# Sums over partitions for modulation rows: float32 matmuls on four column tiles instead of a split pair, and separate buffers for running sum and finished row

## The chip, the core and the metric

The kernel runs on one core of a Trainium2 chip. The metric is the device time of one execution in microseconds (us), as the median of several runs. A core has five engines that work side by side, each through its own queue in order: TensorE (PE in the profile, with its weight loads as PEld), VectorE (DVE), ScalarE (ACT), GpSimd (POOL) and SyncE (SP, which here only issues DMAs).

## The reference, cut to what matters

One layer of a decoder trunk, 512 tokens by 1024 channels, float32. A vector `c` of 1024 values is turned into six rows of 1024 values that shift, scale and gate the activations:

```
cs = silu(c)
mod = cs @ w_ada + b_ada                  # 1024 x 6144 weights
shift1, scale1, gate1, shift2, scale2, gate2 = split(mod, 6)
h = rmsnorm(x, norm1_g) * (1 + scale1) + shift1
...                                       # input projection, two attention mixers, gates
x = x + gate1 * (merged @ w_out)
h2 = rmsnorm(x, norm2_g) * (1 + scale2) + shift2
x = x + gate2 * conv_ffn(h2)
return rmsnorm(x, final_g)
```

The change touches how the last four rows (`gate1`, `shift2`, `scale2`, `gate2`) are computed. The first two are made elsewhere, at the start.

## The kernel before, in words

Most large products are done in three matmuls of a split form: an operand is cut into a rounded high part of type float32r (ScalarE, line 115) and a low part, the rest (VectorE, line 116), and high x high, high x low and low x high are summed in PSUM (lines 119 to 121). That is the helper `split`.

The program runs in stages: normalisation and the first six columns of the input projection (to about 55 us), then both attention mixers with the gate and branch projections (to about 293 us), then the output projection, then the gated MLP with its convolution.

In the second stage the order on TensorE is written out by hand (`manual_schedule` names the tensor engine alone); the order on VectorE, ScalarE, GpSimd and the DMA queues is set by a planner, which puts instructions in order by priority and by when its own model has their inputs and buffers ready. The hand-written order is a chain of attention steps with `fill(n)` between them. One `fill` step is one "tick": it runs one step of the projection at hand (three matmuls), runs what `after(n, ...)` put off by n ticks, and from tick 4 on at every eighth tick advances the generator `ada_rows` by one step.

`ada_rows` computes the four rows in eight halves of 512 columns. A half takes four steps. Each step loads two 128x512 pieces of `w_ada` into a tile `ra` (line 750; it shares four buffers, tag `raw`, with the other weights of this stage) and adds them to a running sum `arow`, each weighted by a column of `cs`: one TENSOR_SCALAR (line 755) for the first piece and one SCALAR_TENSOR_TENSOR (line 757) for each of the other seven. After tick 20 these have a raised priority, below that of the score and softmax instructions and above that of the splits of weights. `arow` has a single buffer (tag `sq2`). After the last piece it holds 128 partial sums per column, one per partition.

What is left is the sum over the 128 partitions. `arow` is split into `arh` and `arl` (lines 115 and 116), and one tick later `ada_spread` multiplies each with a matrix of ones, `onesr`, into a PSUM bank `pr` (lines 766 and 767, 128x512 each), which leaves the sum in every partition. ScalarE copies row 0 back into row 0 of `arow` (line 769), and GpSimd issues a DMA that writes it to `mod_rows`, a small tensor in device memory (line 770). `mod_rows` is read back by three loads: row 0 as `g1b` (line 929), used in line 967 to weight the output projection; rows 1 and 2 as columns (line 940); row 3 as `g2b` (line 929), late in the MLP.

Other names that the steps touch: `sd` (scores and probabilities of the differential attention, maxima in line 673, exponentials in line 687, combined in lines 690 to 693), `td` (their transposes, line 702), `aTh` and `aTl` (the transposes split, lines 430 and 431), `od` (the product with the values), `pA` and `ta` (a branch projection and its merge, line 796), `oa` (line 604: the product of the sliding-window attention with its values, float32 matmuls whose two heads use columns 0 to 63 and 64 to 127 of the array, that is two column tiles).

Of the kernel before, what the change touches and what calls it, by code (L numbers as in the profile page):

```python
# [8 lines left out]
F32 = mybir.dt.float32  # L9
F32R = mybir.dt.float32r  # L10
# [4 lines left out]
P = 128  # L15
D = 1024
S = 512
# [12 lines left out]
ADA_LAG = 1  # L30
# [23 lines left out]
def kernel(  # L54
# [22 lines left out]
    nc = tc.nc  # L77
# [3 lines left out]
    def pool(name, bufs=1, space=None, stack=ctx):  # L81
        kw = {} if space is None else {"space": space}
        return stack.enter_context(tc.tile_pool(name=name, bufs=bufs, reuse_waits="tile", **kw))

    cpool = pool("const")
    big = pool("big")
# [3 lines left out]
    def bank(tag, bufs, shape, name, dt=F32):  # L90
        return ps.tile(shape, dt, tag=tag, bufs=bufs, name=name)
# [7 lines left out]
    def tbank(name, shape=(P, S)):  # L99
        return bank("t", 2, list(shape), name)  # L100
# [4 lines left out]
    def raw_tile(shape, name):  # L105
        return wp.tile(shape, F32, tag="raw", bufs=4, name=name)
# [7 lines left out]
    def split(hi, lo, src):  # L114
        nc.scalar.copy(hi, src)
        nc.vector.tensor_sub(lo, src, hi.bitcast(F32))
# [14 lines left out]
    ones = cpool.tile([P, P], F32, name="ones")  # L131
# [1 line left out]
    warm = cpool.tile([P, 1], F32, name="warm")  # L133
    nc.vector.memset(warm, 0.0)
    nc.scalar.activation(warm, warm, AF.Exp)
    onesr = cpool.tile([P, P], F32R, name="onesr")
    nc.vector.tensor_copy(onesr, ones)
    mhalf = cpool.tile([P, 4], F32, name="mhalf")
    nc.gpsimd.memset(mhalf, -0.5)
    qsc = cpool.tile([P, 4], F32, name="qsc")  # L140
# [105 lines left out]
    ac, mods, wts = {}, {}, {}  # L246
# [269 lines left out]
    def after(n, fn):  # L516
        later.append([n, fn])
# [223 lines left out]
    mod_rows = tc.dram_tile([4, D], F32, name="mod_rows")  # L741

    def ada_rows():
        for idx in range(4):
            for hf in range(2):
                c0 = (2 + idx) * D + hf * S
                ac = big.tile([P, S], F32, tag="sq2", name=f"arow{idx}{hf}")
                for k in range(0, KT, 2):
                    r = raw_tile([P, 2, S], f"ra{idx}{hf}_{k}")
                    nc.sync.dma_start(r, wada[k * P : (k + 2) * P, c0 : c0 + S].rearrange("(a p) n -> p a n", p=P))  # L750
                    with tc.high_priority(offset=HP // 2) if tick[0] > ADA_EASY else ExitStack():
                        for a in range(2):
                            cc = cs[:, k + a : k + a + 1]
                            if k + a == 0:
                                nc.vector.tensor_scalar_mul(ac, r[:, a], cc)
                            else:
                                nc.vector.scalar_tensor_tensor(ac, r[:, a], cc, ac, ALU.mult, ALU.add)  # L757
                    yield
                ah = big.tile([P, S], F32R, tag="g2b0", name=f"arh{idx}{hf}")
                al = big.tile([P, S], F32R, tag="g2b1", name=f"arl{idx}{hf}")  # L760
                split(ah, al, ac)
                after(ADA_LAG, lambda idx=idx, hf=hf, ac=ac, ah=ah, al=al: ada_spread(idx, hf, ac, ah, al))

    def ada_spread(idx, hf, ac, ah, al):
        pr = tbank(f"pr{idx}{hf}")
        nc.tensor.matmul(pr, onesr, ah, start=True, stop=False)
        nc.tensor.matmul(pr, onesr, al, start=False, stop=True)
        row = ac[0:1, :]
        nc.scalar.copy(row, pr[0:1, :])  # L769
        nc.gpsimd.dma_start(mod_rows[idx : idx + 1, hf * S : (hf + 1) * S], row)  # L770


    pair_w = {}
# [26 lines left out]

    pairs, firsts, scored, probs, aTs = {}, {}, {}, {}, {}
    ada = ada_rows()
    add_head(0)
    add_head(1)
# [38 lines left out]
    for s in range(4 * DIFF_HEADS):  # L843
        h, n = divmod(s, NT)
# [621 lines left out]
    for i, (J, name) in enumerate(slots):  # L1466
# [21 lines left out]
        if i in rows_at:  # L1488
            hf = rows_at[i]
# [297 lines left out]
```

## Time and profile before

| what | value |
|---|---|
| median of 3 runs | 706.98 us (706.82 to 708.46) |
| the profiled execution | 708.24 us |
| its span, first to last instruction | 705.4 us |
| mean granted TensorE clock | 0.994 |
| second stage, 55 to 293 us | 238 us, PE busy 235.9 |
| the eight halves: first line 755, last line 770 | 68.4 us, 294.4 us |

The profile shows one execution. Busy time is per engine. A matmul's record includes its way through the pipeline, so records overlap and the distance between starts is the better measure of what one costs. A groups' line has line, engine, operation, output and inputs with shape, and then durations; a wait's line has who waited, for whom, total us, times, and the longest. In a timeline the first two columns are start and duration, and brackets behind a line hold the idle time before it and what ended it.

### The profile page before, as it was taken

What the parts mean: (1) busy time and instruction counts of PE and PEld (TensorE: products, weight loads), DVE (VectorE), ACT (ScalarE), POOL (GpSimd) and SP (SyncE); (2) the same over time, 40 slices, a digit from 0 to 9 for tenths busy, and PEclk for the clock granted to TensorE, in tenths of its full rate; (3) what the DMA queues carried; (4) which work ended last, traced back from release to release, by engine and by line L of the source; (5) the groups of instructions that cost most, each with busy time, mean ns of one, the idle gap of its engine ahead of it and who ended that gap; (6) DMA issues with size and microseconds to landing.
All of it is one profiled execution on the core that took longest, in us unless ns stands there. A gap on an engine that the chain in (4) does not pass through costs nothing. (4 is left out here: it accounts for less than half of the span.)

```text
span 705.4 us, 11197 instructions
## 1 busy us (share of the span) xinstructions
PE 685.0 (97%) x4155; PEld 597.1 (85%) x4155; DVE 578.4 (82%) x1107; ACT 383.9 (54%) x676; POOL 82.2 (12%) x100
## 2 busy tenths in 40 slices
PE   6999999999999999999999999999999999999994
PEld 6777777777787888888889999999999999888884
DVE  5998968788985766773579899888888999979996
ACT  3646766545543333431468656555555666656664
POOL 3000000000011000000030111111101102530300
PEclk9999999999999999999999999999999999999998
DMA  9983624263543774529617888786979748996803
GB/s 311 302 262 98 201 61 154 67 199 90 170 153 100 262 214 142 186 93 288 187 33 148 197 199 204 177 209 182 208 204 230 164 143 204 197 200 191 158 0 119
DMA packets 115861, 121.80 MB, mean 173 GB/s; under 512 B 4415, under 2 KB 93280, under 8 KB 115808
## 3 DMA queue, kind: packets, MB, share of 16 engines
q1 hardware_dynamic: 96894, 95.09, 42.7%
q0 software_dynamic: 18720, 25.73, 21.6%
q8 instruction: 32, 0.52, 0.3%
q10 hardware_dynamic: 194, 0.28, 0.1%
q14 instruction: 21, 0.17, 0.1%
HBM read 118.97 MB, written 2.11 MB: 172 GB/s over the span
## 5 line engine op out<-in xcount | busy, mean ns | idle before, releaser
L1126 PE MATMUL up<-t,m_whi 128*128 128x256 f32 x528 | 96.1, 283 | 0.0
L1126 PEld LDWEIGHTS up<-t,m_whi 128*128 128x128 f32 x528 | 82.3, 192 | 0.0
L1126 PE MATMUL up<-t,m_wlo 128*128 128x256 f32 x264 | 74.7, 283 | 0.1
L1126 PE MATMUL up<-bh,p_wlo 128*128 128x256 f32 x232 | 65.7, 284 | 0.7 <-DVE p_wlo L1069 0.7
L1126 PE MATMUL up<-bh,p_whi 128*128 128x256 f32 x232 | 65.6, 283 | 0.0
L1126 PE MATMUL up<-bl,p_whi 128*128 128x256 f32 x232 | 65.6, 283 | 0.0
L1126 PEld LDWEIGHTS up<-t,m_wlo 128*128 128x128 f32 x264 | 50.6, 192 | 0.3 <-DVE m_wlo L1069 0.3
L1126 PEld LDWEIGHTS up<-bh,p_wlo 128*128 128x128 f32 x232 | 44.5, 192 | 1.1 <-DVE p_wlo L1069 1.1
L1126 PEld LDWEIGHTS up<-bh,p_whi 128*128 128x128 f32 x232 | 44.5, 192 | 0.0
L1126 PEld LDWEIGHTS up<-bl,p_whi 128*128 128x128 f32 x232 | 44.5, 192 | 0.0
L757 DVE SCALAR_TENSOR_TENSOR arow<-ra,cs,arow 128x512 f32<-128x512 f32 x56 | 41.9, 747 | 2.6 <-DMA ra<-in_w_ada_dram 1.8
L1037 POOL DMA_DIRECT2D s<-in_w_up_dram x21 | 27.0, 1361 | 142.9 <-DMA s<-in_w_up_dram 78.0
L1069 DVE TENSOR_TENSOR m_wlo<-s,m_whi 128x1024 fp32r<-128x1024 f32 x31 | 37.7, 1217 | 2.0 <-ACT m_whi L1065 2.0
L1065 ACT CAST m_whi<-s 128x1024 fp32r<-128x1024 f32 x31 | 32.5, 1047 | 9.4 <-DVE s L1059 5.9
L1126 PE MATMUL up<-t,p_whi 128*128 128x256 f32 x176 | 32.2, 283 | 0.0
L687 ACT ACTIVATE sd<-sd,dmx 128x128 f32<-128x128 f32 (+3 forms) x32 | 17.8, 556 | 23.2 <-DVE dmx L685 15.9
L175 POOL TENSOR_TENSOR r<-ms,mhalf 128x1 f32<-128x1 f32 (+1 forms) x16 | 13.2, 828 | 144.7 <-DVE ms L173 74.0
L1126 PEld LDWEIGHTS up<-t,p_whi 128*128 128x128 f32 x176 | 27.4, 192 | 0.2 <-issue 0.2
L1133 ACT ACTIVATE gT<-a,cv 128x512 f32<-128x512 f32 x22 | 17.7, 813 | 17.6 <-DVE a L1168 17.3
L770 POOL DMA_DIRECT2D mod_rows<-arow x8 | 4.3, 540 | 193.7 <-ACT arow L769 193.5
L1065 ACT CAST p_whi<-wa 128x1024 fp32r<-128x1024 f32 x18 | 18.7, 1041 | 12.0 <-PE up L1126 7.2
L1126 PE MATMUL up<-t,p_wlo 128*128 128x256 f32 x88 | 24.9, 283 | 0.0
(478 smaller groups left out, 2073.0 us busy)
## 6 DMA issues: line engine op xcount, KB each, us to landing
ra<-in_w_ada_dram SPq DMA_DIRECT2D x32, 512.0 KB, 4.2
wa<-in_w_up_dram SPq DMA_DIRECT2D x22, 512.0 KB, 4.6
s<-in_w_up_dram SPq DMA_DIRECT2D x21, 512.0 KB, 5.1
s<-in_w_up_dram POOLq DMA_DIRECT2D x21, 512.0 KB, 7.0
adaw<-in_w_ada_dram SPq DMA_DIRECT2D x16, 512.0 KB, 4.9
w<-in_w_in_dram SPq DMA_DIRECT2D x12, 512.0 KB, 4.1
a<-in_w_up_dram SPq DMA_DIRECT2D x11, 512.0 KB, 4.8
b<-in_w_down_dram SPq DMA_DIRECT2D x10, 512.0 KB, 4.7
```

The source lines that it names most:

```text
L175: nc.gpsimd.tensor_tensor(r0, ms, mhalf[:, :n], ALU.pow)
L687: nc.scalar.activation(pm[m], pm[m], AF.Exp, bias=mx[:, m : m + 1], scale=slope, accum_out=lsum[:, m : m + 1])
L757: nc.vector.scalar_tensor_tensor(ac, r[:, a], cc, ac, ALU.mult, ALU.add)
L770: nc.gpsimd.dma_start(mod_rows[idx : idx + 1, hf * S : (hf + 1) * S], row)
L1037: nc.gpsimd.dma_start(dst, upblock(*blk), accum_op=ALU.add)
L1065: nc.scalar.copy(W[J, name][0], R[J, SRC[name]])
L1069: nc.vector.tensor_sub(lo, R[J, SRC[name]], hi.bitcast(F32))
L1126: nc.tensor.matmul(o[u], w[:, k, cu], b[:, k], start=name in ("p1", "m5", "p2") and k == 0 and x == 0, stop=k == 3 and x == 2, skip_group_ ...
L1133: nc.scalar.activation(grow(j), av[J][:, u], AF.Identity, bias=cv[:, 66 + j : 67 + j], scale=cv[:, 44 + j : 45 + j])
```

## The change

The running sum is summed over the partitions without a split. Four float32 matmuls, one for each 128 columns of the half, use 32 columns of the ones matrix as weights and write to a quarter of the partitions of one 128x128 bank: partitions 32g to 32g+31 all hold columns 128g to 128g+127 of the half. `tile_position=(0, 32 * g)` puts each on a column tile of its own. The copy takes the whole 128x128 bank into a tile `row` of its own, and the DMA takes partitions 0, 32, 64 and 96 of it, 128 values each. The running sum alternates between two buffers, tags `sq2` and `g2b1`; `row` has the tag `g2b0`. These two tags held `arh` and `arl` before. The matrix `onesr` goes.

```
-    onesr = cpool.tile([P, P], F32R, name="onesr")
-    nc.vector.tensor_copy(onesr, ones)
...
-                ac = big.tile([P, S], F32, tag="sq2", name=f"arow{idx}{hf}")
+                ac = big.tile([P, S], F32, tag=("sq2", "g2b1")[hf], name=f"arow{idx}{hf}")
...
-                ah = big.tile([P, S], F32R, tag="g2b0", name=f"arh{idx}{hf}")
-                al = big.tile([P, S], F32R, tag="g2b1", name=f"arl{idx}{hf}")
-                split(ah, al, ac)
-                after(ADA_LAG, lambda idx=idx, hf=hf, ac=ac, ah=ah, al=al: ada_spread(idx, hf, ac, ah, al))
-
-    def ada_spread(idx, hf, ac, ah, al):
-        pr = tbank(f"pr{idx}{hf}")
-        nc.tensor.matmul(pr, onesr, ah, start=True, stop=False)
-        nc.tensor.matmul(pr, onesr, al, start=False, stop=True)
-        row = ac[0:1, :]
-        nc.scalar.copy(row, pr[0:1, :])
-        nc.gpsimd.dma_start(mod_rows[idx : idx + 1, hf * S : (hf + 1) * S], row)
+                after(ADA_LAG, lambda idx=idx, hf=hf, ac=ac: ada_spread(idx, hf, ac))
+
+
+    def ada_spread(idx, hf, ac):
+        pr = tbank(f"pr{idx}{hf}", (P, P))
+        for g in range(4):
+            gs = slice(32 * g, 32 * g + 32)
+            nc.tensor.matmul(
+                pr[gs], ones[:, gs], ac[:, g * P : (g + 1) * P], start=True, stop=True, tile_position=(0, 32 * g)
+            )
+        row = big.tile([P, P], F32, tag="g2b0", name=f"row{idx}{hf}")
+        nc.scalar.copy(row, pr)
+        nc.gpsimd.dma_start(
+            mod_rows[idx, hf * S : (hf + 1) * S].rearrange("(g n) -> g n", g=4), row[0:P:32]
+        )
```

## The prediction, made before the change was run

> **What bounds the kernel now.** I read the page's totals first, then the busy time by stage, then single rows.
>
> ```profile
> PE 685.0 (97%) x4155; PEld 597.1 (85%) x4155; DVE 578.4 (82%) x1107; ACT 383.9 (54%) x676; POOL 82.2 (12%) x100
> ```
>
> ```profile
> 55.00:293.00 238.00, 235.89 (x1259) 187.86 (x1258) 184.47 (x457) 121.80 (x273) 11.78 (x16) 1.00 0.50 153
> ```
>
> The second is the stage in which all changed work lies (first arow operation 68.4 us, last row copy 293.5 us); its columns are start and end, length, busy time and count of PE, PEld, DVE, ACT and POOL, granted clock, DMA share and GB/s. PE is busy for 235.9 of 238 us at a clock of 1.00. DVE has 53.5 us free there, ACT 116. So what DVE and ACT save counts only where PE waits for them. A busy PE can still issue late (a 128x512 matmul is shown for 0.39 us, the next starts after 0.23), so I also took the starts of the matmul records, and from each distance to the next the ordinary one (columns at 2.4 per ns plus 0.0135 us, which gives 0.227 for 512). Over 55 to 293 us 11.5 us remain. Most is small change at switches between kinds of matmul; four holes are waits for data: 1.30 us after 143.44, 0.35 after 164.10, 0.49 after 212.55 and 0.74 after 214.57, together **2.9 us**. That is all that a faster DVE or ACT can win here.
>
> After 293 us, PE follows a hand-written order, DVE is 30% busy around 325 us, and the chain of waits begins only at 357 us. The last row is written by 296 us and read at 481.8. A shift at 293 us is therefore passed on whole, and nothing else is changed.
>
> **The change part by part.**
>
> *The matmuls on PE.* Today's pair stands in a stream of ordinary matmuls:
>
> ```profile
> 192.74 0.40 PE L121 MATMUL pga<-hThA,wga_l 128*128 128x512 f32 x1
> 192.97 0.39 PE L766 MATMUL pr<-arh,onesr 128*128 128x512 f32 x1
> 193.20 0.39 PE L767 MATMUL pr<-arl,onesr 128*128 128x512 f32 x1
> 193.44 0.40 PE L119 MATMUL pga<-hThA,wga_h 128*128 128x512 f32 x1
> ```
>
> From the start of the first pr matmul to that of the next unit 193.44 - 192.97 = 0.47 us, no more than two ordinary matmuls. Eight times: 3.7 us leave PE.
>
> What comes is four float32 matmuls with 32 weight columns and 128 moving columns. The nearest row is L604, float32 on two column tiles of 64:
>
> ```profile
> 77.89 0.39 PE L121 MATMUL pw<-hThA,w_l 128*128 128x512 f32 x1
> 78.21 1.73 PE L604 MATMUL oa<-pT,va 128*64 128x256 f32 x16
> 79.87 0.50 PE L119 MATMUL pw<-hThA,w_h 128*128 128x512 f32 x1
> 80.21 0.40 PE L120 MATMUL pw<-hTlA,w_h 128*128 128x512 f32 x1
> ```
>
> Its eight matmul calls stand in the trace as 16 records: a float32 matmul is two passes. The two tiles' records start together (78.475 and 78.480, 78.690 and 78.697), a pass of 256 columns follows the last after 0.216 us, one of 128 after 0.109. So the stream is 6 x 0.216 + 2 x 0.109 = 1.51 us. From 77.89 to 80.21 are 2.32 us; less two ordinary intervals of 0.23 that leaves 1.86, so going into column tiles and back costs 1.86 - 1.51 = **0.35 us**: 0.09 before the first record, some 0.05 in the first pass, the rest behind the last.
>
> With four tiles side by side the new group is 2 x 0.109 + 0.35 = 0.57 us, 0.10 more than today; eight times **+0.8 us**. No row shows four tiles at once. The lower end is that both passes hide in the switch, 0.40, which is -0.06 x 8 = -0.5 us. A middle end is that records go no faster than the fastest pairs of load and matmul that the trace has, one per 0.055 us (those of L604): 8 x 0.055 + 0.35 = 0.79, +0.32 x 8 = +2.6 us. The upper end is eight passes one after another: 8 x 0.109 + 0.35 = 1.22, +0.75 x 8 = +6.0 us. I take +0.8, since L604 is the only float32 column-tile row and its tiles do run together. The Trainium skill, "TensorEngine Tiling (Array Packing)", Key Properties, says that a change of tiling mode drains TensorE, which speaks against this change; the trace agrees, with 0.35 us. "TensorE: Matmul & The Clock Gate" there, Measured speedup vs the span model, has 2.38 times from three column tiles, 79% of ideal; by an estimate from that page, four would stream in 0.218 / 0.79 = 0.28 us and the sum here would be +1.2 in place of +0.8. No run here shows it.
>
> *The split, removed.*
>
> ```profile
> L115 ACT CAST arh<-arow x8: 602/622/624, 83.6 to 284.3; 128x512 fp32r<-128x512 f32 x8
> L116 DVE TENSOR_TENSOR arl<-arow,arh x8: 681/688/693, 87.7 to 285.0; 128x512 fp32r<-128x512 f32 x8
> L769 ACT COPY arow<-pr x8: 562/576/577, 108.9 to 293.5; 1x512 f32<-1x512 f32 x8
> ```
>
> 8 x 0.622 = 5.0 us leave ACT and 8 x 0.688 = 5.5 us leave DVE (durations are min/median/max in ns). The row copy becomes 128 x 128 elements. Its cost goes by elements per partition: a 128x128 cast from PSUM at 145.30 takes 0.27 us, so 8 x (0.576 - 0.27) = 2.4 us more leave ACT. The split was done 7 to 20 us before PE came to it, so PE did not wait for it; all of this is worth nothing but what it opens in the four holes.
>
> *Buffers.* With one arow tile, the next half's first operation waits for the write of the finished row:
>
> ```profile
> DVE arow L755 <- DMA mod_rows<-arow: 5.7, 4, 3.4
> ```
>
> That is 5.7 us in 4 waits on DVE, 3.4 the longest, and behind each, loaded halves pile up and DVE then runs them in a burst. The clearest burst makes the largest hole:
>
> ```profile
> 140.50 0.74 DVE L757 SCALAR_TENSOR_TENSOR arow<-ra,cs,arow 128x512 f32<-128x512 f32 x1
> ...
> 141.84 0.74 DVE L757 SCALAR_TENSOR_TENSOR arow<-ra,cs,arow 128x512 f32<-128x512 f32 x1
> ...
> 143.28 0.74 DVE L757 SCALAR_TENSOR_TENSOR arow<-ra,cs,arow 128x512 f32<-128x512 f32 x1
> ...
> 144.47 0.74 DVE L693 SCALAR_TENSOR_TENSOR sd<-sd,dls,sd 128x128 f32<-128x128 f32 x2
> ```
>
> ```profile
> 144.96 0.30 PE L702 MATMUL td<-ident,sd 128*128 128x128 f32 x1 [1.14 <-DVE sd L693]
> ```
>
> PE's transpose waits for L693, which stands behind L757. With two arow tiles, a half waits for the matmuls of the half before the last, some 25 us earlier, so these four operations run when their ra tiles land. Without the one at 143.28 the hole loses 0.74; without the one at 140.50 too, which delays the maxima that ACT waits for, it can lose all 1.30. I take 1.0. The holes after 212.55 and 214.57 have L115 (0.62 us on ACT at 208.94) and L116 (0.69 on DVE at 209.59) among the work just ahead; of their 1.23 us I take 0.5. What is late next there is ACT's exponentials. The hole after 164.10 I leave. Sum: **-1.5 us**.
>
> New waits: the row copy waits for the write of the row before, landed 20 us earlier (1.6 us to land). Behind L755, if it ever waited for PE, would stand DVE's maxima and splits; PE is long past those matmuls.
>
> *The rest.* The write has four pieces of 512 B in place of one of 2 KB. Its readers are g1b, issued right behind the fifth write and first used at 291.8 (64 us of cover), and the column loads at 251.7, used after 340; 1 us more costs nothing. If the cover were gone, it would be about 1 us once. The onesr cast (0.23 us at 1.11) stands in an idle stretch of DVE before 2.75: nothing. The order of DVE, ACT and the DMA queues in this stage is the planner's, and it can come out otherwise; I set that at 0, with 2.5 us to either side, about the sum of today's holes.
>
> **Sum.** +0.8 - 1.5 = -0.7 us. The profiled execution took 708.24 us around a span of 705.4, 0.2% above the median of 706.98; I carry the difference to the median: **706.3 us**.
>
> **The rivals.**
> *All holes close.* -2.9 + 0.8 = -2.1: 704.9 us. For it: three of four holes have arow work just ahead. Against: at 164.10 it is ACT's exponentials and DVE's own L693 that are late.
> *Four tiles don't run side by side* (slower). Mechanism: the float32 passes of the four tiles queue up at PE. Price: +6.0 - 1.5 = +4.5, 711.5 us; at the rate of the fastest pairs +2.6 - 1.5 = +1.1, 708.1 us. It makes the kernel measurably slower from a group of 0.47 + (2.1 + 1.5) / 8 = 0.92 us on, which is more than 5 of 8 passes in a row. For: two tiles are the most that a row shows. Against: those two cost no more than one.
> *The planner moves the burst.* arow work, now ready early and ahead of the weight splits, makes new holes ahead of PE: +2.5 for the new, nothing won, +0.8: 710.3 us. Against: DVE is 60% busy from 88 to 106 us, where the second half's sums would fall.
> *The buffers do nothing*, as arow operations stay paced by their loads: +0.8 - 0.5 = +0.3, 707.3 us.
>
> **How the numbers follow.** Forecast 0.46; all holes close 0.14; tiles in a row 0.08, pair rate 0.11; planner 0.13; buffers idle 0.08. The range leaves out the full row of tiles, most of the planner's case and the edge of the best: 704.3 to 709.5. A measurement can tell about 0.3%, 2.1 us, so faster means below 704.9: half of the best case, and 0.07 of the forecast's own spread to the planner's gain, 0.14. Slower means above 709.1: the row of tiles and most of the planner's case, 0.19. Same: 0.67.
>
> **What would show it.** The distance from the matmul before pr to the second one after it: 1.03 us instead of 0.93. pr records of four tiles starting within 0.02 us of each other. No DVE wait for mod_rows, and arow operations in pairs. The hole before the transpose near 143 us under 0.4 us. The prediction is wrong if pr groups take over 0.9 us, or if holes of over 1 us appear elsewhere between 55 and 293 us, or if anything after 293 us changes in length.

## The result, and the profile after

The changed kernel takes 710.46 us (median of 7, 709.07 to 712.94), the kernel before 706.97 (median of 7, 706.69 to 708.46). The ratio is 1.0047, 95% interval 1.0033 to 1.0061: **slower by 0.47%**. The forecast was 706.3, with 709.5 as the upper end of its range. The profiled execution took 712.94 us, the longest of the seven, with a span of 711.0. Another execution of the same kernel, traced later as the run `r_after` below, took 708.73 with a span of 706.8.

The totals of the page, after:

```profile
PE 686.1 (96%) x4203; PEld 594.8 (84%) x4203; DVE 572.4 (81%) x1098; ACT 376.8 (53%) x668; POOL 82.2 (12%) x100
```

and the stage of 55 to 293 us in it (start and end, length, then busy time and count of PE, PEld, DVE, ACT and POOL, granted clock, DMA share, GB/s):

```profile
55.00:293.00 238.00, 233.89 (x1289) 183.11 (x1288) 178.82 (x453) 113.17 (x264) 11.86 (x16) 1.00 0.50 151
```

DVE's work is down by 6.0 us and ACT's by 7.1, as intended. PE, which was busy for 235.9 us of this stage, is now busy for 233.9, at the same clock of 1.00. So PE waits more here although the engines that feed it have less to do.

Where the time went is read by matching each matmul of the one trace to the same matmul of the other and following the difference of their starts. In `r_after` it is -0.7 us at 62 us, +2.1 at 284 and +1.5 from 364 on. The +2.8 between 62 and 284 us is the loss. What lies outside varies from run to run: the profiled execution of after is already 2.1 us late at 45 us, `r_after` 0.7 early, in a part where the two programs differ by the `onesr` cast alone.

The holes of PE, taken as the prediction took them (distance to the next matmul less the ordinary one, those over 0.25 us, 55 to 300 us) are these:

| kernel | holes in us, with the time after which each opens | sum |
|---|---|---|
| before | 143: 1.30, 164: 0.35, 213: 0.49, 215: 0.74 | 2.9 |
| after, profiled | 55: 0.27, 127: 0.42, 142: 0.76, 147: 1.27, 188: 0.25, 192: 0.98, 217: 0.87, 220: 0.71 | 5.5 |
| `r_after` | 124: 0.41, 139: 0.65, 144: 1.23, 189: 0.98, 214: 0.88, 217: 0.71 | 4.9 |

The same six holes stand in both executions of the changed kernel, so they belong to its program. All but those at 55 and 220 us are PE's transpose `td` waiting for the probabilities (now line 691 on DVE). DVE's own waits tell why; this is the list of waits in `after` from 55 to 300 us (who waits, for whom, total us, times, longest):

```profile
DVE arow L755 <- DMA ra<-in_w_ada_dram: 22.2, 16, 3.9
...
PE td L700 <- DVE sd L691: 3.5, 5, 1.1
```

The same two waits in the kernel before:

```profile
DVE arow L757 <- DMA ra<-in_w_ada_dram: 1.8, 3, 0.8
...
PE td L702 <- DVE sd L693: 1.6, 3, 1.1
```

DVE also waited 5.7 us in 4 for the write of the row there. That wait is gone, as forecast, but 22.2 us of waits for loads have come. One of them is seen whole in the timeline of `r_after` (start, duration, engine, line; in brackets the idle time before it and what ended it). DVE's lines are complete from 121.71 on; of ACT and PE one line each is shown:

```profile
120.42 0.49 ACT L685 ACTIVATE sd<-sd,dmx 128x256 f32<-128x256 f32 x1
...
121.71 1.54 DVE L755 SCALAR_TENSOR_TENSOR arow<-ra,cs,arow 128x512 f32<-128x512 f32 x2 [2.48 <-DMA ra<-in_w_ada_dram]
123.17 0.22 DVE L688 RECIPROCAL dls<-dls 128x2 f32<-128x2 f32 x2
123.36 0.23 DVE L689 TENSOR_TENSOR dls<-dls,nlam 128x1 f32<-128x1 f32 x2
123.56 0.55 DVE L690 TENSOR_SCALAR sd<-sd,dls 128x128 f32<-128x128 f32 x2
124.02 0.74 DVE L691 SCALAR_TENSOR_TENSOR sd<-sd,dls,sd 128x128 f32<-128x128 f32 x2
...
124.51 0.30 PE L700 MATMUL td<-ident,sd 128*128 128x128 f32 x1 [0.24 <-DVE sd L691]
```

ACT is done with the exponentials of the first two blocks by 121.0 us. DVE could go on with the probabilities, but two running-sum operations stand ahead of them in its queue. They wait 2.48 us for their piece, 0.7 of it after the last exponential, and then take 1.5 us. The first probabilities are done at about 124.5, and PE has its hole of 0.41 us.

The matmuls themselves came out near the forecast. The group in the changed kernel's trace:

```profile
197.21 0.39 PE L121 MATMUL pga<-hThA,wga_l 128*128 128x512 f32 x1
197.53 0.43 PE L764 MATMUL pr<-arow,ones 128*32 128x128 f32 x8
197.88 0.50 PE L119 MATMUL pga<-hThA,wga_h 128*128 128x512 f32 x1
198.22 0.39 PE L120 MATMUL pga<-hTlA,wga_h 128*128 128x512 f32 x1
```

From 197.21 to 198.22 is 1.01 us; the same distance is 0.93 before. Within the group, the four tiles' records of one pass start within 0.02 us, and those of the second pass 0.13 us after the first.

### The profile page after: what moved, and what is told of

It is laid out like the page before. It is cut to its first block, busy times and chain, and to the rows that moved or that the text cites. A ratio compares the mean times of both kernels' runs of the same rounds, so it can differ in the third digit from the quotient of the medians.

```text
span 711.0 us, 11254 instructions
## 1 busy us (share of the span) xinstructions
PE 686.1 (96%) x4203; PEld 594.8 (84%) x4203; DVE 572.4 (81%) x1098; ACT 376.8 (53%) x668; POOL 82.2 (12%) x100
## 5 line engine op out<-in xcount | busy, mean ns | idle before, releaser
L755 DVE SCALAR_TENSOR_TENSOR arow<-ra,cs,arow 128x512 f32<-128x512 f32 x56 | 41.9, 748 | 22.6 <-DMA ra<-in_w_ada_dram 22.2
L769 POOL DMA_DIRECT2D mod_rows<-row x8 | 4.9, 612 | 212.3 <-ACT row L768 212.3
```

The lines of the kernel that those rows point to most:

```text
L769: nc.gpsimd.dma_start(mod_rows[idx, hf * S : (hf + 1) * S].rearrange("(g n) -> g n", g=4), row[0:P:32])
```

## The experiments

Five causes were weighed. A: the second buffer. B: the new matmuls and row path. C: time lost outside the stage (it fell already with the second trace, above). D: the running-sum operations and their waits in DVE's queue. E: the planner, which writes the queues of DVE and ACT anew when an instruction is changed, and wrote a worse order. The table has all times; each ratio is to the kernel before on the same chip. Holes are summed from 55 to 300 us, as above.

| run | time, us | ratio, 95% interval | holes, us |
|---|---|---|---|
| `e1_single` | 712.53 | 1.0083 [1.0069, 1.0097] | 8.1 |
| `e2_two` | 714.88 | 1.0124 [1.0105, 1.0142] | 9.4 |
| `e3_noprio` | 710.47 | 1.0056 [1.0043, 1.0068] | 6.2 |
| `e4_ahead` | 713.62 | 1.0096 [1.0080, 1.0111] | 8.3 |
| `e5_nosum` | 709.62 | 1.0036 [1.0024, 1.0048] | 4.6 |
| `e6_noread` | 719.00 | 1.0166 [1.0152, 1.0180] | 9.0 |
| `e8_pin` | 713.18 | 1.0085 [1.0068, 1.0103] | 7.8 |
| `e9_pinb` | 710.74 | 1.0049 [1.0037, 1.0061] | 5.6 |
| `e10_hold` | 706.49 | 0.9996 [0.9986, 1.0007] | 2.8 |
| `e12_holdsq` | 706.60 | 0.9993 [0.9983, 1.0003] | 3.1 |
| `e11_swap` | 730.90 | 1.0340 [1.0322, 1.0358] | 20.0 |
| `r_after` | 709.46 | 1.0041 [1.0027, 1.0055] | 4.9 |
| `e13_rest` | 714.04 | 1.0096 [1.0072, 1.0119] | 9.1 |
| `e14_sums` | 708.52 | 1.0026 [1.0016, 1.0037] | 4.6 |
| `e15_moved` | 709.70 | 1.0042 [1.0025, 1.0058] | 5.9 |

### One part of the change at a time

`e1_single` is the changed kernel with one buffer for the sums.

```
-                ac = big.tile([P, S], F32, tag=("sq2", "g2b1")[hf], name=f"arow{idx}{hf}")
+                ac = big.tile([P, S], F32, tag="sq2", name=f"arow{idx}{hf}")
```

> The changed kernel with one buffer for the running sum (tag sq2 for both halves), all else as changed. Theory A (order on DVE): the second buffer lets the planner put running-sum operations early in DVE's queue, where they wait for their own loads (22 us in 16 waits after the change, 1.8 in 3 before) and hold up the softmax behind them; with one buffer those waits fall under 6 us, the PE holes between the first stage's end and the output projection fall from 5.3 us back to about 2.9 or less, and the time is 706.5 to 708 us. Theory B (the new sum itself: column tiles, 128-row copy, write in four pieces): still 709.5 to 711 us, holes over 4.5 us. Theory C (the loss lies outside this stage, in the first 45 us, where the profiled execution lost 2.1 us, and in late loads around 345 us): between 709 and 710.5 us with the holes gone.

It took 712.53 us, 2 more than the change and above what any of the theories gave. **A alone fell**: taking the second buffer away doesn't give the time back. Its waits for `ra` are half as long (11.0 us in 8), and yet the hole ahead of `od` at 217 us is 2.18 us, where the changed kernel has 0.71.

`e2_two` is the kernel before with two buffers; the low part is left out, and the high part is multiplied twice so that PE has the same work.

```
-                ac = big.tile([P, S], F32, tag="sq2", name=f"arow{idx}{hf}")
+                ac = big.tile([P, S], F32, tag=("sq2", "g2b1")[hf], name=f"arow{idx}{hf}")
...
-                split(ah, al, ac)
+                nc.scalar.copy(ah, ac)
...
-        nc.tensor.matmul(pr, onesr, ah, start=True, stop=False)
-        nc.tensor.matmul(pr, onesr, al, start=False, stop=True)
+        for _ in range(2):
+            nc.tensor.matmul(pr, onesr, ah, start=True, stop=True)
```

> The kernel before with two buffers for the running sum (tags sq2 and g2b1); to free the second, the low part of the split is left out (the pair of 128x512 matmuls runs on the high part twice, the second overwriting the first, so the rows are sums of rounded values), and the pair, the one-row copy and the write stay. PE has the same matmuls as before; DVE has 8 x 0.69 us less. Theory A: waits of the running sum for its loads over 15 us in all, PE holes about 5 us, 708.5 to 710.5 us although nothing was added on PE. Theory B: 705.5 to 707.3 us. Theory C: within 1 us of before, or slower with the loss in the first 45 us.

714.88 us, without a column tile in it and above the ranges of A and B. A loss of this kind needs no new matmul, which speaks against **B**; what the new matmuls cost in the changed kernel itself shows only when the order is held, below. Half of A did come: with two buffers the sums wait 29.8 us for their loads here too (25.5 in 16 at line 757, 4.3 in 2 at line 755). So the second buffer lets the planner place the sums where they wait, but it isn't all of the loss.

### The running sums and their loads

`e3_noprio` takes away the raised priority of the loads and sums; `e4_ahead` traces each load one step earlier than its sums.

```
-                    with tc.high_priority(offset=HP // 2) if tick[0] > ADA_EASY else ExitStack():
+                    with ExitStack():
```

> The changed kernel without the raised priority of the running-sum operations, which then stand behind the weight splits of the same tick. Theory A: they move back in DVE's queue, their loads have landed by then, waits for loads fall under 10 us, PE holes to 3 us or less, 706.5 to 708.5 us, unless weights come late because their buffers are held longer. Theory B: 709.5 to 711 us. Theory C: 709 to 710.5 us.

```
+        ahead = load(0)
+        yield
...
-                    r = raw_tile([P, 2, S], f"ra{idx}{hf}_{k}")
-                    nc.sync.dma_start(r, wada[k * P : (k + 2) * P, c0 : c0 + S].rearrange("(a p) n -> p a n", p=P))
+                    r, n = ahead, 8 * idx + 4 * hf + k // 2 + 1
...
+                    if n < 32:
+                        ahead = load(n)
```

> The changed kernel with each load of the running sum's pieces issued one step (eight ticks) ahead of its use, so that a load has landed when its operations come up; one of the four weight buffers is then always taken. Theory A: waits for these loads under 5 us, PE holes under 3 us, 706 to 708 us; if the lost buffer makes weights late, holes appear at the projections instead, before the first matmul of a unit. Theory B: 709.5 to 711 us. Theory C: 709 to 710.5 us.

Neither helps: 710.47 and 713.62 us, with 25.0 us of waits for `ra` in 13 and 26.5 in 18. `e4_ahead` didn't do what it was made for: from 100 us on its loads go out hardly earlier than the changed kernel's, or not at all (the 11th at 121.4 us where that one has 119.7, the 14th at 146.0 and 146.7).

`e5_nosum` leaves out 56 of the 64 sum operations, 42 us of DVE's work; `e6_noread` lets the sums read a tile that is already there in place of the loaded one, so that no sum waits for a load (its sums are of other data; of the two lines changed the second is shown).

```
-                            else:
-                                nc.vector.scalar_tensor_tensor(ac, r[:, a], cc, ac, ALU.mult, ALU.add)
```

> The changed kernel without 56 of the 64 running-sum operations: only the first piece of each half is scaled, the other seven are loaded and not added (the rows are wrong). Theory D, formed after the first four runs: PE's holes are late transposes td, and these are late because running-sum operations, and their waits for loads, stand in DVE's queue between ACT's exponentials and the operation that combines the probabilities, or ahead of the maxima; in the changed kernel 9 of the 16 blocks lose time so. Without these operations: PE holes over 0.25 us sum to 1.5 us or less (5.3 in the changed kernel, 2.9 before), time 704 to 706 us. Rival, theory E: the planner's order of the rest (weight splits and the wait for GpSimd's power ahead of the probabilities) makes the holes whatever the running sum does: holes 3 us or more, 707.5 us or more.

```
...
-                                nc.vector.scalar_tensor_tensor(ac, r[:, a], cc, ac, ALU.mult, ALU.add)
+                                nc.vector.scalar_tensor_tensor(ac, hTh[k + a].bitcast(F32), cc, ac, ALU.mult, ALU.add)
```

> The changed kernel with all 64 running-sum operations, but reading tiles that already lie in the core (the input hT in place of the loaded weights, so the rows are wrong); the loads are still issued. It takes the wait for the loads away and leaves the operations. Theory D splits: if it is the waits, holes fall to 2 us or less and the time to 705 to 707 us; if it is the operations' own 0.75 us in the way, holes stay at 4 us or more and the time at 709 us or more. Theory E: 708.5 us or more, with the late blocks behind weight splits.

With 42 us less to do on DVE the kernel is still slower than before, 709.62 us. Its largest hole, 2.19 us, has no sum near it. DVE in `e5_nosum`:

```profile
212.40 0.55 DVE L429 TENSOR_TENSOR aTl<-td,aTh 128x384 fp32r<-128x384 f32 x1
212.87 1.22 DVE L116 TENSOR_TENSOR wba_l<-wba,wba_h 128x1024 fp32r<-128x1024 f32 x1
214.00 0.68 DVE L795 SCALAR_TENSOR_TENSOR ta<-ta,pA 128x512 f32<-128x512 f32 x1
214.60 1.22 DVE L116 TENSOR_TENSOR wga_l<-wga,wga_h 128x1024 fp32r<-128x1024 f32 x1
215.74 0.68 DVE L429 TENSOR_TENSOR aTl<-td,aTh 128x512 fp32r<-128x512 f32 x1
```

PE needs the last of these for `od` from 214.3 on and gets it at 216.4. Two weight splits and a merge, 2.9 us, stand between two pieces of the transposed tiles. In `e6_noread` no sum waits for a load, and it takes 719.0 us: 7 of its 12 us are lost before 62 us, where the planner now lays out the first stage otherwise; the rest are holes of PE in the second stage. **D by itself fell**: the sums and their waits make single holes, but in the orders that the planner wrote without them there are others.

`e8_pin` queues each step's sums behind the probabilities last traced (issue order, no wait); `e9_pinb` does the same to the kernel before.

```
-            nc.vector.scalar_tensor_tensor(pm[0], pm[0], lsum[:, 0:1], pm[1], ALU.mult, ALU.add)
+            latest[:] = [nc.vector.scalar_tensor_tensor(pm[0], pm[0], lsum[:, 0:1], pm[1], ALU.mult, ALU.add)]
...
+                    behind_softmax = tc.issue_after(latest[0].ins) if latest else ExitStack()
+                    with behind_softmax, tc.high_priority(offset=HP // 2) if tick[0] > ADA_EASY else ExitStack():
```

> The changed kernel with each step's running-sum operations held, in DVE's queue, behind the last operation of the softmax that was written out last, so that none stands between exponentials and probabilities of that block. Theory D: no block has running-sum work or waits for loads between exponentials and probabilities, holes 2 us or less, 705 to 707.5 us. Theory E: the number of late blocks stays, holes 4 us or more, 709 us or more.

> The kernel before with the same hold. It keeps the pair of matmuls, so a PE group costs 0.47 us and not 0.55. Theory D: the hole of 1.3 us near 143 us, which had two running-sum operations in the way, goes; 705 to 706.5 us. Theory E: the planner's order changes and the time is 708 us or more.

713.18 and 710.74 us, so both get slower. In `e8_pin` the loads of later weights are late instead:

```profile
244.61 0.39 PE L121 MATMUL pA<-outah,wba_l 128*128 128x512 f32 x1
248.67 0.50 PE L119 MATMUL pga<-hThA,wga_h 128*128 128x512 f32 x1 [3.67 <-ACT ta L782]
```

In `e9_pinb` PE comes to `pr` before its sum is split (waits from 55 to 300 us):

```profile
PEld pr L768 <- ACT arh L115: 1.4, 1, 1.4
PEld pr L769 <- DVE arl L116: 1.3, 1, 1.3
```

By now eight kernels with eight different edits were all slower than the one before, by 2.5 to 12 us. Of the five theories that leaves E: the order of before is a good one, and each of these edits lost it. It is so far what is left over, and not shown.

### The order held

The traces show the queues of PE and SP in the same order in both kernels, but for the matmuls that were replaced. At least 77 of DVE's 1098 instructions, 13 of ACT's 670 and one of POOL's stand elsewhere (like instructions can't be told apart, so it may be more). To test E directly, each instruction of the changed kernel is tied behind the one that preceded it in the order of before, in every queue; the ties fix the order of issue and add no wait.

```
+def hold_order(tc):
+    traced = {i.name: i for i in tc.nc.cur_bb.bb.instructions}
...
+        for one, two in zip(names, names[1:]):
+            tc.add_manual_dep(
+                traced[two], one, mybir.DependencyInfo(mybir.DependencyClass.NoSync, mybir.DependencyReason.DATA),
...
         tile_decoder_trunk_kernel(tc, *args)
+        hold_order(tc)
```

> The changed kernel, whole, with every queue (PE, DVE, ACT, POOL, SP) held in the order that the planner had written for the kernel before; only the instructions that the change removed are missing from it. Theory 'order' (the loss is the planner's other order of DVE's and ACT's queues between 120 and 300 us): PE's holes between 55 and 293 us sum to 3.2 us or less (2.9 before, 5.3 after) and the time is 706.0 to 708.0 us. Theory 'the new work itself' (column tiles, second buffer, row tile, faster sums colliding with the loads): 709.5 to 711.5 us, holes 4.5 us or more, as in the changed kernel with its own order.

**706.49 us, the time of before, with the whole change in it.** The holes are those of before (143: 1.10, 163: 0.50, 212: 0.49, 214: 0.74). Its waits from 55 to 300 us:

```profile
DVE arow L755 <- DMA ra<-in_w_ada_dram: 2.8, 4, 1.1
...
PE td L700 <- DVE sd L691: 1.6, 3, 0.9
```

The 22.2 us of waits for loads are 2.8, with the same loads in the same order on SP. The block that showed the 2.48 us wait now runs so on DVE:

```profile
119.50 0.16 DVE L683 TENSOR_SCALAR dmx<-dmx 128x2 f32<-128x2 f32 x1
119.58 0.75 DVE L755 SCALAR_TENSOR_TENSOR arow<-ra,cs,arow 128x512 f32<-128x512 f32 x1
120.24 0.17 DVE L683 TENSOR_SCALAR dmx<-dmx 128x2 f32<-128x2 f32 x1
120.61 0.17 DVE L688 RECIPROCAL dls<-dls 128x2 f32<-128x2 f32 x1 [0.21 <-ACT sd L685]
```

The sum's piece is there, it runs while ACT does its exponentials, and DVE's next wait, 0.21 us, is for those. **E is shown** as the cause of the loss: the same instructions take the time of before in the order of before, and from 62 to 284 us the difference to before grows by 0.07 us here and by 2.8 in `r_after`, the changed kernel's own order on the same chip. Of these 2.7 us, 2.0 are in the holes (2.8 and 4.9) and the rest in gaps of under 0.25 us.

`e12_holdsq` is the same with one buffer (the edit of `e1_single` with the order held).

> As the run before it, with one buffer for the running sums in place of two, in the same held order. What is left of the change is the column tiles and the row tile. If the second buffer is worth something of its own once the order is fixed, DVE waits for the row's matmuls again and this is 0.3 to 1.5 us slower than with two; if it is worth nothing, both agree within 0.3 us. Theory 'order': 706.0 to 708.5 us; theory 'the new work itself': 711 us or more (712.5 with the planner's own order).

706.60 us. The two differ by 0.1 us, well inside both intervals, so at one order the second buffer is worth nothing. `e1_single`, the same kernel in the planner's order, took 5.9 us more (on another chip).

`e11_swap` goes the other way: the kernel before, held in the changed kernel's order except for its sums and splits.

> The other way round: the kernel before, with every queue held in the changed kernel's order, except for the running sums and their splits, which stay free, since the one buffer can't follow the changed kernel's order of them. Theory 'order': 708.5 to 712 us, PE's holes 4 us or more. Theory 'the new work itself': 706.5 to 707.5 us, holes about 2.9 us.

730.9 us, slower as E has it but far outside the 708.5 to 712 that were expected. The largest hole:

```profile
251.94 0.39 PE L121 MATMUL pA<-outah,wba_l 128*128 128x512 f32 x1
257.29 0.79 PE L119 MATMUL pga<-hThA,wga_h 128*128 128x512 f32 x1 [4.97 <-ACT ta L779]
```

Ahead of that `ta`, ACT sat idle for 4.21 us until the load of `wbd` landed; it was held to split `wbd` first. So this run shows that the order matters, not how much of the change's 3 us it explains.

`r_after`, the changed kernel again, took 709.46 us, just under what was expected, with the holes at the same places.

> The changed kernel again, for a second trace beside the three: 709.5 to 711 us, PE's holes between 55 and 293 us 4.5 to 6 us at the same places (126, 142, 147, 192, 217 us). If the holes lie elsewhere, they come from the execution and not from the order of the queues.

### Which part of the order

`e13_rest` holds all but the 64 sums; `e14_sums` holds only sums, maxima and probabilities on DVE and leaves the rest free; `e15_moved` is `e10_hold` with 8 sums taken from between a block's maxima and its probabilities and queued behind them.

> The changed kernel with every queue held in the order of the kernel before, but for the 64 operations of the running sums, which the planner places itself (it puts them about where the changed kernel has them: three of them between the exponentials and the probabilities of the first two blocks). Reason 'the places of the sums' (the sums stand between a block's maxima and its probabilities, and wait there for their loads): 708.5 to 710.5 us, PE's holes between 55 and 293 us over 4 us. Reason 'the places of the rest' (weight splits, transposed-copies and softmax steps against each other): 706 to 707.5 us, holes about 3 us.

> The other half: only DVE's running sums, maxima and probabilities are held against each other in the order of the kernel before; all else is left to the planner, which sets 30 places of DVE and ACT otherwise than in the kernel before. Reason 'the places of the sums': 706 to 707.5 us, holes about 3 us. Reason 'the places of the rest': 708.5 to 710.5 us, holes over 4 us.

> The changed kernel with every queue held in the order of the kernel before, but for 8 running-sum operations, which stood between a block's maxima and its probabilities and are queued behind the probabilities here. Both reasons agree on this: the hole of 1.1 us at 142.7 us, whose block has three of them (1.9 us) ahead of its probabilities, should shrink to 0.3 us or less; the time falls by 0.5 to 1.2 us, to 705.3 to 706.0 us, a ratio of 0.998 to 0.999, at the edge of what can be told. If a row's matmuls then wait for their sum (around 162 us), 0.5 us of it is lost again.

714.04, 708.52 and 709.70 us. `e13_rest` lies above both of its ranges and is worse than leaving all to the planner; `e14_sums` lies where the places of the rest were to put it. Neither half is enough. They don't divide the loss cleanly either: the sums of `e14_sums`, though held against the softmax, still wait 14.0 us in 9 for their loads, where `e10_hold` has 2.8 in 4. What "the rest" does is seen in `e14_sums` ahead of its largest hole (1.22 us at 184.81):

```profile
181.93 0.15 DVE L169 TENSOR_SCALAR ms<-pss 128x4 f32<-128x4 f32 x1
183.25 0.16 DVE L181 TENSOR_TENSOR rt<-r 128x4 f32<-128x4 f32 x1 [1.16 <-POOL r L173]
...
183.75 1.23 DVE L116 TENSOR_TENSOR wba_l<-wba,wba_h 128x1024 fp32r<-128x1024 f32 x1
184.89 0.68 DVE L671 CUSTOM_DVE_ANT_0 sd<-sd,ddf 128x512 f32<-128x512 f32 x1
185.50 0.08 DVE L671 DVE_READ_ACCUMULATOR2_ANT dmx<- 128x1 f32 x1
185.50 0.61 DVE L691 SCALAR_TENSOR_TENSOR sd<-sd,dls,sd 128x384 f32<-128x384 f32 x1
```

A small normalisation step waits 1.16 us for GpSimd, and a weight split of 1.23 us follows, both ahead of the probabilities that PE waits for. The kernel before has them behind.

`e15_moved` was expected at 705.3 to 706.0 and missed by 4 us. The hole at 143 us did go, but between 157 and 167 us holes of 4.0 us stand where `e10_hold` has 0.5. They begin with a load of weights that comes late. In `e15_moved`:

```profile
153.22 1.05 ACT L115 CAST w_h<-w 128x1024 fp32r<-128x1024 f32 x1 [5.60 <-DMA w<-in_w_in_dram]
...
154.30 1.23 DVE L116 TENSOR_TENSOR w_l<-w,w_h 128x1024 fp32r<-128x1024 f32 x1 [2.64 <-ACT w_h L115]
155.44 0.16 DVE L683 TENSOR_SCALAR dmx<-dmx 128x2 f32<-128x2 f32 x1
```

and the same three in `e10_hold`:

```profile
149.57 1.05 ACT L115 CAST w_h<-w 128x1024 fp32r<-128x1024 f32 x1 [1.34 <-DMA w<-in_w_in_dram]
...
150.67 1.22 DVE L116 TENSOR_TENSOR w_l<-w,w_h 128x1024 fp32r<-128x1024 f32 x1
151.81 0.16 DVE L683 TENSOR_SCALAR dmx<-dmx 128x2 f32<-128x2 f32 x1
```

The moved sums read their pieces later, and a piece holds one of the four `raw` buffers until then: SP waits for the sums, 5.4 us at the longest. The next two pieces go out at 144.33 and 145.90 us in place of 140.30 and 143.08, and the weights `w` behind them in SP's queue at 147.55 in place of 145.79. These take 5.6 us to land in place of 3.8. ACT splits them 3.65 us later, DVE's split waits for that, and the maxima `dmx` stand behind the split. So moving 8 sums on DVE made a load late, and the load made the softmax late. No kernel was found that beats both.

## Why the prediction was wrong, point by point

**The step that failed** is "The order of DVE, ACT and the DMA queues in this stage is the planner's, and it can come out otherwise; I set that at 0". The order of DVE and ACT did come out otherwise (that of the loads on SP did not), and this is worth 3.0 us: on one chip the changed kernel takes 709.46 us in its own order and 706.49 in the old one. With the 710.46 of the first measurement, which was not taken beside it, it is 4.0. The range held 2.5 us to either side for it, about the sum of the holes of before, and the new holes alone sum to 4.9.

The rival "the planner moves the burst" gave 710.3 us at a chance of 0.13 and is nearest in time and in kind. Its mechanism is half right. It had the sums ready early; in the trace they stand early in DVE's queue and are not ready, so DVE waits 22.2 us for loads with the probabilities queued behind. And it had the sums alone in the way, where `e5_nosum`, almost without sums, is still slower than before. The argument against the rival, that DVE is only 60% busy from 88 to 106 us (67% by the trace, 12.07 of 18 us), counts busy time, and what came was waiting time.

**The holes** were forecast to lose 1.5 of 2.9 us, and grew to 4.9. Of the signs set down, holes of over 1 us elsewhere came (1.27 us after 147), and the hole of under 0.4 us near 143 did not. In the old order the holes are 2.8: the arow operations ahead of the hole at 143 us are held in their places there. Where 8 sums are moved (`e15_moved`), that hole closes as worked out, and more opens behind.

**The matmuls** were right in mechanism. In six of the eight places the distance is 1.01 to 1.02 us against 0.93 before, +0.08, where 1.03 was forecast. In the other two, in the old order, the group costs nothing more: behind the third, PE waits for the probabilities either way, and the fifth stands behind the small matmuls of line 725 (0.87 against 0.89). There the eight sum to +0.45 us, where +0.8 was forecast. All eight records of a group start within 0.15 us, four tiles within 0.02, and the rivals in which they queue up are out. From the Trainium skill, "TensorE: Matmul & The Clock Gate", Measured speedup vs the span model, the prediction had estimated +1.2 us in all, a group of 0.63 us; it is not borne out, as 1.01 less two ordinary intervals of 0.23 is 0.55. What the Trainium skill says in "TensorEngine Tiling (Array Packing)", Key Properties, of a drain at a change of tiling mode agrees with the trace: the extra time lies around the group (below).

**The wait for the row's write** is gone (5.7 us in 4), as forecast. It was worth nothing: `e10_hold` and `e12_holdsq` are without it and take the time of before. **The split** was worth nothing too, as forecast. **The row copy** takes 0.266 us where 0.27 was forecast, and nothing was lost after 293 us that another execution confirms.

**The sum**, 706.3, agrees with `e10_hold` at 706.49, but by luck and not by its terms: the matmuls add about half of their +0.8, the -1.5 of the holes is not there, and the time is within the scatter of the kernel before.

## What to carry to other kernels

Where a planner writes the queues, an edit has two prices: that of its instructions, and that of the new order that all others get. In a kernel whose busiest engine is 99% busy in a stage, the second can be the larger (here 3 us against 0.45), and work taken from other engines need not offset it (here 6.0 us of DVE's and 7.1 of ACT's). Hold the old order and run the change once in it: what is left is the change itself, and the rest is the order. The other way round it failed here, since the old kernel did not fit the new order (730.9 us).

## What the runs showed of the hardware

Inside the group the four column tiles are faster than what they replace: from the first `pr` record to the next ordinary matmul are 0.356 us, where two ordinary matmuls of 512 columns took 0.47. The price lies around it: 0.32 us from the matmul before it to its first record in place of 0.23, and 0.34 in place of 0.23 behind it. The wait ahead of the group goes with the tiles and not with the type float32: in the kernel before, the float32 matmuls of line 725, on the whole array, start 0.23 us after the ordinary matmul ahead of them, those of line 604, on two column tiles, 0.32.

DVE's queue held what stood behind a waiting instruction although that was ready: a 2.48 us wait for a load and the two sums it held up delayed probabilities whose inputs were there by 121.0 us until 123.2.
